# Transformer layers on one core: x and the first weights loaded in order of use, key products ahead of the compression, three gate tiles inside the last merge

## The chip, the cores and the metric

The kernel runs on one core of a Trainium2 chip. The metric is device time in microseconds (us) of one execution, the median of several runs.

## The reference, cut to what matters

Two transformer blocks follow each other over one sequence of 512 tokens with 1024 features, all in float32.

```python
def first_block(x, ...):                       # D = 1024, S = 512
    h = rms_norm(x, attn_norm_w)
    x = x + token_mixer(h, ...)                # retention, short convolution, sparse attention
    h = rms_norm(x, ffn_norm_w)
    x = x + conv_glu_ffn(h, ...)
    return rms_norm(x, final_norm_w)

def nsa_attention(...):                        # the sparse attention of the token mixer
    kc = compress(kc_raw, cmp_pos[0], cmp_w1[0], cmp_w2[0])   # blocks of 32 keys -> one
    vc = compress(vc_raw, cmp_pos[1], cmp_w1[1], cmp_w2[1])
    # heads attend to kc/vc, to selected keys ks/vs, and to a window kw/vw

def second_block(x, ...):
    h = rms_norm_2(x, attn_norm)
    # y_dn: gated delta rule branch; y_swa: sliding window branch
    gates = sigmoid(gate_raw)                  # 2 x 1024 columns: 16 tiles of 128
    merged = gates[0] * (y_dn @ w_branch_dn) + gates[1] * (y_swa @ w_branch_swa)
    x = x + merged @ w_out
    return x + (silu(h2 @ w_gate) * (h2 @ w_up)) @ w_down
```

## The kernel before, in words

Activations are held feature-major: 128 features on the partitions, 512 tokens in a row, eight such tiles for 1024 features. Every product runs in float32r as three matmuls, on a high and a low part of each factor: `split` makes the high part on ScalarE (ACT, L269 or L272) and the low part on VectorE (DVE, L270 or L273). `weight` loads a weight tile over SyncE's (SP's) queue (L286) and splits it; the loaded tile `wf` has two buffers, its parts `wh` and `wl` have three. A `gemm` is eight weight tiles of 128 by 128, with three matmuls each (wh·xh, wh·xl, wl·xh): 24 matmuls of 512 columns on TensorE (PE). RMS norm is applied behind a product: R, a row broadcast of 1/rms, multiplies the results.

The program is written in order of computation, and a scheduler under the kernel orders every engine's instructions ahead of time; each engine then works through its own list in that order. Tiles come from pools with a fixed number of buffers: in PSUM two each of `g`, `s` and `t`, and one each of `o` and `o2`. A load through `load` is issued by GpSimd (POOL) and keeps its place behind the last matmul written before it.

`setup` loads the norm vectors `vecs` and half of x over ACT's queue, the other half of x over POOL's, and the first weight tile in two halves over SP's. It splits x by tile, with the norm's weight as scale, computes the sum of squares (ACT squares, DVE adds to `acc`, PE sums the columns with `ones`), and `finish_norm` makes R of it through the reciprocal square root on DVE (L341 to L350) and four PE transposes (L372). The first product `nsa_raw_keys` has four gemms (the raw keys and values to be compressed, `w_kcvc`); for each result, ACT and DVE copy four half tiles into K2 (L486, L487).

Then come `nsa_compress` (per side 16 additions on DVE at L458, twice 16 small matmuls into `o`, a gelu on ACT and DVE at L465 to L472 whose result `zz` feeds a last small product) and `nsa_keys` (four gemms `w_kswk`, then the token-major products for the values, `w_vs` and `w_vw`).

In the second block `gates2` computes the 16 gate tiles (gemm, times R, tanh) into units of memory: 8 and 9 ahead of the delta rule, 10 to 15 behind its scan, and two behind each pair of the eight sliding-window heads (0 to 7). `merge` then runs twice. Per tile it has a gemm of half depth (12 matmuls, 256 KB of weights), DVE multiplies it by the gate (L841) and POOL adds it to `merged` in the second merge (L842). `split_all` splits merged (L272, L273) for the product with `w_wo`.

Of the kernel before, what the change touches and what calls it, by code (L numbers as in the profile page):

```python
# [8 lines left out]
F32 = mybir.dt.float32  # L9
# [3 lines left out]
OP = mybir.AluOpType  # L13
# [12 lines left out]
PITCH = 8 * (16 * 128 + 16)  # L26

# [169 lines left out]
class Kern:  # L197
# [92 lines left out]

    def gemm(self, w, xh, xl, nk=KD, p=None):
# [117 lines left out]
    def setup(self):  # L409
        nc, A = self.nc, self.A  # L410
        self.vecs = self.cp.tile([128, V_N], F32, name="vecs")
        nc.scalar.dma_start(self.vecs, A["vecs"])
        x = self.units(KD)
        for k in range(KD):
            (nc.scalar if k % 2 else nc.gpsimd).dma_start(x(k), A["xT"][:, k, :])
        first = self.weight(A["w_kcvc"][0], 2)
# [4 lines left out]
        for k in range(KD):  # L421
            self.split(xh(k), xl(k), x(k), self.vec(NORM1 + k))
        self.xh, self.xl = xh, xl
        self.consts = {}
        self.load_consts(0)
        self.load_consts(1)
        self.rows = self.cp.tile([128, R_N - R_DNO], F32, name="rows")
        self.load(self.rows, A["rows"][:, R_DNO:R_N].to_broadcast([128, R_N - R_DNO]))
# [46 lines left out]
    def nsa_raw_keys(self):  # L475
        nc, A = self.nc, self.A
        self.K2, self.cw = [], []
        for which in range(2):
            K = self.unit(shape=(128, 4, 512))
            for pair in range(2):  # L480
                p = self.gemm(A["w_kcvc"][which * 2 + pair], self.xh, self.xl, KD, self.pss() if which else None)
                t = self.scaled(p)
                for s in range(2):
                    rows = slice(64 * s, 64 * s + 64)
                    g = 2 * pair + s
                    nc.scalar.activation(K[0:64, g, :], t[rows, :], AF.Copy)  # L486
                    nc.vector.tensor_copy(K[64:128, g, 0:511], t[rows, 1:512])  # L487
# [35 lines left out]
    def nsa_keys(self):  # L523
# [913 lines left out]
```

## Time and profile before

| what | value |
|---|---|
| median of 3 runs | 2039.32 us (2038.29 to 2039.98) |
| the profiled execution | 2040.16 us |
| its span | 2038.4 us |
| PE busy | 2009.6 us |
| DVE busy | 1206.2 us |
| ACT busy | 837.6 us |
| POOL busy | 227.6 us |

The span runs from the first to the last recorded instruction of the profiled execution; 1.8 us of its time lie around it. PE is busy for nearly all of it, so the rows to look at are those in front of which PE stood still, and those of the engine that it waited for. In a timeline a row holds: start (us), length (us), engine, line, operation, what is written from what, shape, count, and in brackets the idle time before it and what ended that.

### The profile page before, as it was taken

What the parts mean: (1) busy time and instruction counts of PE and PEld (TensorE: products, weight loads), DVE (VectorE), ACT (ScalarE), POOL (GpSimd) and SP (SyncE); (2) the same over time, 40 slices, a digit from 0 to 9 for tenths busy, and PEclk for the clock granted to TensorE, in tenths of its full rate; (3) what the DMA queues carried; (4) which work ended last, traced back from release to release, by engine and by line L of the source; (5) the groups of instructions that cost most, each with busy time, mean ns of one, the idle gap of its engine ahead of it and who ended that gap; (6) DMA issues with size and microseconds to landing.
All of it is one profiled execution on the core that took longest, in us unless ns stands there. A gap on an engine that the chain in (4) does not pass through costs nothing.

```text
span 2038.4 us, 26002 instructions
## 1 busy us (share of the span) xinstructions
PE 2009.6 (99%) x9800; PEld 1669.1 (82%) x9800; DVE 1206.2 (59%) x2250; ACT 837.6 (41%) x1514; POOL 227.6 (11%) x336
## 2 busy tenths in 40 slices
PE   7999999999999999999999999999999999999999
PEld 6888888888888888888888888879878878888887
DVE  7477887854525645467767544784576764444322
ACT  4466776742122323334444332643544332232211
POOL 3000000000201111111111100011000211111100
PEclk9999999999999999999999999999999999999999
DMA  6122111122242232443333343321221353323442
GB/s 236 54 73 62 43 43 62 53 82 95 93 119 77 74 102 83 123 156 95 93 104 94 116 137 110 104 81 48 83 64 42 102 176 94 103 93 96 127 124 78
DMA packets 61837, 193.33 MB, mean 95 GB/s; under 512 B 10909, under 2 KB 13221, under 8 KB 61200
## 3 DMA queue, kind: packets, MB, share of 16 engines
q1 hardware_dynamic: 54336, 166.32, 26.5%
q0 software_dynamic: 6656, 24.17, 3.7%
q8 instruction: 77, 1.26, 0.2%
q10 hardware_dynamic: 720, 1.19, 0.2%
q14 instruction: 48, 0.39, 0.1%
HBM read 182.07 MB, written 9.58 MB: 94 GB/s over the span
## 4 chain that ended last, share of the span: by engine, by line
PE 89%; DVE 5%; ACT 3%; DMA 2%; issue 1%; ACTq 0%; POOL 0%; SPq 0%; DVEq 0%
PE g L263 73%; PE o L263 5%; PE s L263 5%; PE t L263 2%; PE t L676 2%; DVE wl L270 1%; ACT wh L269 1%; DMA u<-in_xT 1%; DVE st L573 0%; DVE sm L635 0%; DVE u L273 0%; DVE w L440 0%; ACT PT L665 0%; PE t L1334 0%; PE t L728 0%
## 5 line engine op out<-in xcount | busy, mean ns | idle before, releaser
L263 PE MATMUL g<-u,wh 128*128 128x512 f32 x4464 | 1402.2, 392 | 11.9 <-ACT u L272 10.1
L263 PEld LDWEIGHTS g<-u,wh 128*128 128x128 f32 x4464 | 834.6, 188 | 181.2 <-ACT u L272 11.2
L263 PE MATMUL g<-u,wl 128*128 128x512 f32 x2232 | 874.5, 392 | 0.2 <-DVE wl L270 0.2
L269 ACT ACTIVATE wh<-wf 128x1024 fp32r<-128x1024 f32 (+3 forms) x325 | 331.7, 1021 | 812.9 <-PE g L263 572.5
L270 DVE TENSOR_TENSOR wl<-wf,wh 128x1024 fp32r<-128x1024 f32 (+3 forms) x325 | 403.3, 1241 | 214.6 <-ACT wh L269 211.2
L263 PEld LDWEIGHTS g<-u,wl 128*128 128x128 f32 x2232 | 420.0, 188 | 84.5 <-DVE wl L270 1.2
L405 DVE TENSOR_TENSOR w<-g,R 128x512 f32<-128x512 f32 x104 | 71.5, 688 | 113.3 <-PE g L263 113.2
L440 DVE SCALAR_TENSOR_TENSOR w<-w,vecs 128x510 f32<-128x510 f32 (+1 forms) x140 | 104.6, 747 | 3.2 <-ACT w L438 0.8
L263 PE MATMUL o<-u 128*128 128x256 f32 (+1 forms) x418 | 78.0, 288 | 2.3 <-issue 1.4
L263 PE MATMUL g<-wh,u 128*128 128x512 f32 (+3 forms) x320 | 79.9, 330 | 0.0
L263 PE MATMUL s<-u,st 128*128 128x256 f32 (+2 forms) x288 | 73.3, 342 | 0.3 <-DVE mn L635 0.2
L263 PEld LDWEIGHTS o<-u 128*128 128x128 f32 x418 | 61.1, 189 | 12.8 <-ACT u L269 4.5
L269 ACT ACTIVATE u<-t 128x512 fp32r<-128x512 f32 (+1 forms) x112 | 56.1, 531 | 23.0 <-PE t L676 10.4
L1367 POOL TENSOR_TENSOR w<-w,R 128x512 f32<-128x512 f32 x22 | 39.0, 1773 | 198.5 <-ACT w L1366 198.5
L272 ACT ACTIVATE u<-w 128x512 fp32r<-128x512 f32 x44 | 27.4, 624 | 77.9 <-POOL w L889 77.9
L273 DVE SCALAR_TENSOR_TENSOR u<-w,u 128x512 fp32r<-128x512 f32 x44 | 30.4, 690 | 47.7 <-ACT u L272 47.7
L263 PEld LDWEIGHTS g<-wh,u 128*128 128x128 f32 x320 | 54.8, 189 | 4.2 <-DVE w L745 0.3
L263 PEld LDWEIGHTS s<-u,st 128*128 128x128 f32 x288 | 46.7, 189 | 10.4 <-issue 3.9
L263 PE MATMUL g<-wl,u 128*128 128x512 f32 (+3 forms) x160 | 52.6, 329 | 0.0
L438 ACT ACTIVATE w<-w,vecs 128x512 f32<-128x512 f32 x64 | 46.2, 722 | 13.8 <-DVE w L405 13.3
L889 POOL TENSOR_TENSOR w<-w 128x512 f32<-128x512 f32 x22 | 28.3, 1288 | 208.7 <-DVE w L440 208.7
L861 DVE TENSOR_TENSOR st<-st,g 128x512 f32<-128x512 f32 x24 | 16.5, 688 | 44.1 <-PE g L263 44.1
(388 smaller groups left out, 2036.8 us busy)
## 6 DMA issues: line engine op xcount, KB each, us to landing
wf<-in_w_fu SPq DMA_DIRECT2D x44, 512.0 KB, 3.5
wf<-in_x_gu SPq DMA_DIRECT2D x44, 512.0 KB, 3.6
wf<-in_w_sc SPq DMA_DIRECT2D x24, 512.0 KB, 3.5
wf<-in_w_mg SPq DMA_DIRECT2D x24, 512.0 KB, 3.5
wf<-in_w_fd SPq DMA_DIRECT2D x16, 512.0 KB, 3.7
wf<-in_x_gt SPq DMA_DIRECT2D x16, 512.0 KB, 3.5
wf<-in_x_dn SPq DMA_DIRECT2D x16, 512.0 KB, 3.7
x<-st POOLq DMA_DIRECT2D x24, 256.0 KB, 2.4
```

What stands on the lines that cost most here:

```text
L263: self.last = self.nc.tensor.matmul(out, l, r, start=start, stop=stop)
L269: nc.scalar.activation(hi, src, AF.Copy)
L270: nc.vector.tensor_sub(lo, src, hi.bitcast(F32))
L272: nc.scalar.activation(hi, src, AF.Copy, scale=scale)
L273: return nc.vector.scalar_tensor_tensor(lo, src, scale, hi.bitcast(F32), op0=OP.mult, op1=OP.subtract)
L405: self.nc.vector.tensor_mul(t, p, self.R)
L438: nc.scalar.activation(dst, src, AF.Copy, scale=self.vec(w + (nt - 1) * stride + j))
L440: nc.vector.scalar_tensor_tensor(dst[:, i:], src[:, :T - i], self.vec(w + (nt - 1 - i) * stride + j), dst[:, i:], op0=OP.mult, op1=OP.add)
L676: nc.tensor.transpose(pt[:, c:c + 128], parts[v][:, k * 128:(k + 1) * 128], self.ident)
L861: nc.vector.tensor_add(r, r, p)
L889: nc.gpsimd.tensor_mul(a, a, v)
L1367: nc.gpsimd.tensor_mul(t, t, self.R)
```

## The change

`setup`: only the eight columns of the first norm's weights (`n1`) are loaded over ACT's queue. x goes over SP's queue together with the first weight tile, in order of use: first half of the weight, x tiles 0 to 2, second half, x tiles 3 to 7. The splits are written in the same order. `vecs`, the constants and `rows` are loaded over POOL's queue behind a small copy that waits for the low part of x tile 4.

`block1`: `nsa_keys` (its four gemms) stands ahead of `nsa_compress`; the token-major products are now `nsa_values`, behind it. The second copy into K2 moves from DVE to ACT.

`block2`: after the scan only gates 10 to 12 are computed; the window heads take 13 to 15 and 0 to 4; gates 5, 6 and 7 are computed inside the second merge. In that merge the last three additions go to DVE in place of POOL.

```diff
+    def weight_x(self, ap, load, split):
...
+        halves = slice(0, 512), slice(512, 1024)
+        for c, ks in zip(halves, ((0, 1, 2), (3, 4, 5, 6, 7))):
+            self.nc.sync.dma_start(wf[:, c], ap[:, c])
+            load(ks)
+        for c, ks in zip(halves, ((0, 1, 2), (3, 4, 5, 6, 7))):
+            self.split(wh[:, c], wl[:, c], wf[:, c])
+            for k in ks:
+                split(k)
+        return wh, wl
...
     def setup(self):
-        nc.scalar.dma_start(self.vecs, A["vecs"])
+        nc.scalar.dma_start(n1, A["vecs"][:, NORM1:NORM1 + KD])
         x = self.units(KD)
-        for k in range(KD):
-            (nc.scalar if k % 2 else nc.gpsimd).dma_start(x(k), A["xT"][:, k, :])
-        first = self.weight(A["w_kcvc"][0], 2)
+        xd = lambda ks: [nc.sync.dma_start(x(k), A["xT"][:, k, :]) for k in ks]
...
-        for k in range(KD):
-            self.split(xh(k), xl(k), x(k), self.vec(NORM1 + k))
+        first = self.weight_x(A["w_kcvc"][0], xd, lambda k: self.split(xh(k), xl(k), x(k), n1[:, k:k + 1]))
...
+        self.last = nc.gpsimd.tensor_copy(self.vecs[:, 0:1], xl(4)[:, 0:1].bitcast(F32))
+        self.load(self.vecs, A["vecs"], self.last)
...
     def nsa_raw_keys(self):
-                    nc.vector.tensor_copy(K[64:128, g, 0:511], t[rows, 1:512])
+                    nc.scalar.activation(K[64:128, g, 0:511], t[rows, 1:512], AF.Copy)
...
     def merge(self, gates, out_w, yh, yl, merged, first, nk=KD):
-                nc.gpsimd.tensor_add(merged(n), merged(n), th)
+                add = nc.vector if nk < KD and n >= LATE else nc.gpsimd
+                add.tensor_add(merged(n), merged(n), th)
...
     def block1(self):
         self.nsa_raw_keys()
+        self.nsa_keys()
         self.nsa_compress()
-        self.nsa_keys()
+        self.nsa_values()
...
     def gates2(self, g, ns):
-            if n % 8 == 0:
-                self.gu = self.units(8)
+            if n in (0, 8):
+                self.gu = self.units(8 if n else LATE)
...
     def block2(self, x2, acc, acc2):
-        self.gates2(gates, range(10, 16))
+        self.gates2(gates, range(10, 13))
...
-            self.gates2(gates, range(2 * j, 2 * j + 2))
+            self.gates2(gates, ((13, 14), (15, 0), (1, 2), (3, 4))[j])
...
-        self.merge(lambda n: gates[n], A["x_bd"], yh, yl, merged, False, 4)
+        self.merge(lambda n: gates[n] if n < LATE else self.gate(A["x_gt"][n]), A["x_bd"], yh, yl, merged, False, 4)
```

LATE is 5. Three places show what moves. The first is SP's list at the start of the program (wf is the loaded weight tile, u a tile of x). Before:

```order
L286 DMA wf<-in_w_kcvc 128x512 x2
L286 DMA wf<-in_w_kcvc 128x1024 x3
L286 DMA wf<-in_w_kswk 128x1024 x4
L286 DMA wf<-in_w_vs 128x1024 x2
L286 DMA wf<-in_w_vw 128x912 x2
```

And now:

```order
L300 DMA wf<-in_w_kcvc 128x512
L431 DMA u<-in_xT 128x512 x3
L300 DMA wf<-in_w_kcvc 128x512
L431 DMA u<-in_xT 128x512 x5
L287 DMA wf<-in_w_kcvc 128x1024 x3
```

All eight tiles of x have moved into this queue, ahead of the second weight tile.

The second is PE's list at the first half of the compression (`o<-u` are its first 16 matmuls of one half, `o<-zz,st` its last product; `g<-u,wh` belongs to a gemm of the key products, `g<-wh,u` to the token-major product `w_vs`). Before:

```order
L263 MATMUL g<-u,wh 128x512
L263 MATMUL o<-u 128x128 x16
L263 MATMUL g<-u,wh 128x512
L263 MATMUL g<-u,wl 128x512
L263 MATMUL o<-u 128x128 x16
L263 MATMUL g<-u,wh 128x512 x2
...
L263 MATMUL o<-zz,st 128x128 x2
```

And now:

```order
L264 MATMUL o<-u 128x128 x16
L264 MATMUL g<-wh,u 128x256
L264 MATMUL g<-wl,u 128x256
L264 MATMUL g<-wh,u 128x256 x2
L264 MATMUL o<-u 128x128 x16
L264 MATMUL g<-wl,u 128x256
L264 MATMUL g<-wh,u 128x256 x2
L264 MATMUL g<-wl,u 128x256
L264 MATMUL o<-zz,st 128x128
```

It stood in the second key gemm; it now stands at the start of `w_vs`, with all four key gemms ahead of it.

The third is DVE's list at the end of the second merge (`wl` is a weight split, `u<-u,s`, `w<-w,s` the product with the gate, `w<-g,R` the new gate's scaling, `u<-u,w` the addition, `u<-u` the low part of merged, `st` belongs to the product behind it). Before:

```order
L270 TENSOR_TENSOR wl<-wf,wh 128x1024
L841 SCALAR_TENSOR_TENSOR u<-u,s 128x512
L273 SCALAR_TENSOR_TENSOR u<-u 128x512
L270 TENSOR_TENSOR wl<-wf,wh 128x1024
L273 SCALAR_TENSOR_TENSOR u<-u 128x512
L1401 SCALAR_TENSOR_TENSOR st<-st,vecs,R_10286 128x512
```

And now:

```order
L422 TENSOR_TENSOR w<-g,R 128x512
L271 TENSOR_TENSOR wl<-wf,wh 128x1024
L862 SCALAR_TENSOR_TENSOR w<-w,s 128x512
L274 SCALAR_TENSOR_TENSOR u<-u 128x512
L864 TENSOR_TENSOR u<-u,w 128x512
L271 TENSOR_TENSOR wl<-wf,wh 128x1024
L274 SCALAR_TENSOR_TENSOR u<-u 128x512
```

The addition has joined DVE's list between the last product with the gate and the last low part.

## Rows read from the trace of the kernel before

**Rows 1.** The page's first part: busy time, share of the span, instructions.

```profile
PE 2009.6 (99%) x9800; PEld 1669.1 (82%) x9800; DVE 1206.2 (59%) x2250; ACT 837.6 (41%) x1514; POOL 227.6 (11%) x336
```

**Rows 2.** Who PE waited for, whole span: total us, times, longest us.

```profile
PE g L263 <- ACT u L272: 10.1, 3, 8.3
...
PE o L263 <- DVE PT L1338: 0.7, 1, 0.7
...
PE o L263 <- ACT PT L1340: 0.4, 1, 0.4
```

**Rows 3.** Timeline of the start, all engines (the columns are explained above).

```profile
5.57 0.63 ACT L269 ACTIVATE wh<-wf 128x512 fp32r<-128x512 f32 x1 [0.40 <-DMA wf<-in_w_kcvc]
...
15.36 0.72 ACT L272 ACTIVATE u<-u,vecs 128x512 fp32r<-128x512 f32 x1 [1.63 <-DMA u<-in_xT]
...
16.11 0.75 DVE L273 SCALAR_TENSOR_TENSOR u<-u,vecs 128x512 fp32r<-128x512 f32 x1 [1.56 <-ACT u L272]
...
24.22 1.48 DVE L385 TENSOR_TENSOR acc<-acc,sm 128x512 f32<-128x512 f32 x2
...
25.76 1.05 PE L263 MATMUL o<-ones,acc 128*128 128x1 f32 x8 [0.77 <-DVE acc L385]
...
29.04 0.16 DVE L350 SCALAR_TENSOR_TENSOR rsr<-rsa,rsy 128x4 f32<-128x4 f32 x1
...
31.99 0.61 PE L263 MATMUL s<-u,wh 128*128 128x512 f32 x2
...
35.39 0.61 PE L263 MATMUL s<-u,wh 128*128 128x512 f32 x2
```

**Rows 4.** Two stretches of the start; the last two columns are DMA share and GB/s.

```profile
2.30:5.30 3.00, 0.00 (x0) 0.00 (x0) 0.34 (x3) 1.91 (x2) 2.96 (x7) 1.00 0.98 325
...
9.00:13.50 4.50, 4.50 (x14) 3.05 (x14) 3.11 (x6) 3.07 (x5) 0.00 (x0) 1.00 1.03 393
```

**Rows 5.** Tile wf, first 45 us: ns min/median/max, first and last start.

```profile
L269 ACT ACTIVATE wh<-wf x8: 629/1050/1069, 4.5 to 36.8; 128x1024 fp32r<-128x1024 f32 x6, 128x512 fp32r<-128x512 f32 x2
L270 DVE TENSOR_TENSOR wl<-wf,wh x8: 692/1218/1226, 5.2 to 39.0; 128x1024 fp32r<-128x1024 f32 x6, 128x512 fp32r<-128x512 f32 x2
L286 SPq DMA_DIRECT2D wf<-in_w_kcvc x5: 327/387/424, 0.8 to 18.3; - x5
```

**Rows 6.** DMA issues: count, KB each, median us from issue to landing.

```profile
wf<-in_x_bs SPq DMA_DIRECT2D x8, 256.0 KB, 2.6
```

**Rows 7.** Timeline of the compression, all engines.

```profile
44.70 4.02 PE L263 MATMUL o<-u 128*128 128x128 f32 x32 [1.44 <-issue]
...
62.33 3.84 PE L263 MATMUL o<-u 128*128 128x128 f32 x32 [0.43 <-ACT w L465]
...
64.27 0.23 DVE L472 TENSOR_SCALAR zz<-w 128x128 f32<-128x128 f32 x1
...
67.46 0.73 PE L263 MATMUL g<-u,wh 128*128 128x512 f32 x2 [0.49 <-DVE w L535]
```

**Rows 8.** Timeline of the copies into K2, ACT.

```profile
32.24 2.56 ACT L486 ACTIVATE u<-w 64x512 f32<-64x512 f32 x4
```

**Rows 9.** A stretch inside `w_vs` and `w_vw`: us, PE busy (count), PEld busy.

```profile
85.00:104.00 19.00, 19.00 (x144) 19.00 (x143) 5.63 (x9) 6.97 (x13) 0.00 (x0) 1.00 0.18 56
```

**Rows 10.** Timeline of the second merge's end, all engines.

```profile
1628.35 0.67 DVE L841 SCALAR_TENSOR_TENSOR u<-u,s 128x512 f32<-128x512 f32 x1
...
1629.12 1.65 POOL L842 TENSOR_TENSOR u<-u 128x512 f32<-128x512 f32 x1 [1.22 <-DVE u L841]
...
1631.48 0.50 PE L263 MATMUL g<-u,wh 128*128 128x512 f32 x1 [1.06 <-ACT u L272]
...
1632.51 0.50 PE L263 MATMUL g<-u,wh 128*128 128x512 f32 x1 [0.53 <-DVE u L273]
```

**Rows 11.** Two stretches behind it; the third column from the end is the granted clock.

```profile
1632.50:1636.30 3.80, 3.79 (x10) 2.98 (x11) 3.33 (x5) 2.30 (x3) 1.08 (x2) 0.60 0.72 251
1636.30:1640.30 4.00, 4.00 (x18) 3.27 (x17) 0.43 (x1) 0.11 (x1) 0.00 (x0) 0.95 0.70 208
```

More of the change, by code (lines that the diff above doesn't have):

```diff
@@ L26 @@
 PITCH = 8 * (16 * 128 + 16)
+LATE = 5
 NORM1, NORM_F1, NORM_FIN, NORM2, NORM_F2 = 0, 8, 16, 24, 32
@@ L289, in weight @@
         return wh, wl
+    def weight_x(self, ap, load, split):
+        ap = ap.rearrange("p k c -> p (k c)")
+        wf = self.wp.tile([128, 1024], F32, name="wf", bufs=2)
+        wh = self.wp.tile([128, 1024], F32R, name="wh", bufs=3)
+        wl = self.wp.tile([128, 1024], F32R, name="wl", bufs=3)
+        halves = slice(0, 512), slice(512, 1024)
[7 more added lines that the diff above has]
+        return wh, wl
     def gemm(self, w, xh, xl, nk=KD, p=None):
@@ L410, in setup @@
         nc, A = self.nc, self.A
-        self.vecs = self.cp.tile([128, V_N], F32, name="vecs")
-        nc.scalar.dma_start(self.vecs, A["vecs"])
+        n1 = self.cp.tile([128, KD], F32, name="n1")
+        nc.scalar.dma_start(n1, A["vecs"][:, NORM1:NORM1 + KD])
         x = self.units(KD)
-        for k in range(KD):
-            (nc.scalar if k % 2 else nc.gpsimd).dma_start(x(k), A["xT"][:, k, :])
-        first = self.weight(A["w_kcvc"][0], 2)
+        xd = lambda ks: [nc.sync.dma_start(x(k), A["xT"][:, k, :]) for k in ks]
         self.ones = self.cp.tile([128, 1], F32, name="ones")
@@ L420, in setup @@
         acc = self.accum()
-        for k in range(KD):
-            self.split(xh(k), xl(k), x(k), self.vec(NORM1 + k))
+        self.vecs = self.cp.tile([128, V_N], F32, name="vecs")
+        self.rows = self.cp.tile([128, R_N - R_DNO], F32, name="rows")
+        first = self.weight_x(A["w_kcvc"][0], xd, lambda k: self.split(xh(k), xl(k), x(k), n1[:, k:k + 1]))
         self.xh, self.xl = xh, xl
         self.consts = {}
[L425 to L428, printed above, removed]
+        self.last = nc.gpsimd.tensor_copy(self.vecs[:, 0:1], xl(4)[:, 0:1].bitcast(F32))
+        self.load(self.vecs, A["vecs"], self.last)
+        for c in range(2):
+            self.load_consts(c)
+        self.load(self.rows, A["rows"][:, R_DNO:R_N].to_broadcast([128, R_N - R_DNO]), self.last)
         self.ident = self.const("ident")
@@ L521, in nsa_compress, with nsa_values, ev, ev_s @@
         self.pbuf, self.pn = ((b[1], b[2]), (b[0], b[3])), 0
+    def nsa_values(self):
+        nc, A = self.nc, self.A
+        xh, xl = self.xh, self.xl
+        self.V = [self.unit(F32R, (128, 4, 4, 128)) for _ in range(2)]
+        self.gates = self.cp.tile([128, 4, 48], F32, name="gates")
+        def ev(br, t, p):
+            src = p[:, :256].rearrange("p (g d) -> p g d", g=4)
+            hi, lo = self.V[br][:, t, :, 0:64], self.V[br][:, t, :, 64:128]
+            r = self.r[:, t:t + 1]
+            nc.scalar.activation(hi, src, AF.Copy, scale=r)
+            nc.vector.scalar_tensor_tensor(lo, src, r, hi.bitcast(F32), op0=OP.mult, op1=OP.subtract)
+        def ev_s(t, p):
+            ev(0, t, p)
+        def ev_w(t, p):
+            ev(1, t, p)
+            nc.scalar.activation(self.gates[:, t, :], p[:, 256:304], AF.Tanh, scale=self.rh[:, t:t + 1])
+        self.gemm_nat(A["w_vs"], 256, xh, xl, ev_s)
+        self.gemm_nat(A["w_vw"], 304, xh, xl, ev_w)
+        nc.vector.tensor_scalar(self.gates, self.gates, 0.5, 0.5, op0=OP.mult, op1=OP.add)
+        self.y = self.units(8)
     def nsa_keys(self):
@@ L541, in nsa_keys @@
                     nc.vector.tensor_sub(KL[rows, s, :], t[rows, :], KH[rows, s, :].bitcast(F32))
-        self.V = [self.unit(F32R, (128, 4, 4, 128)) for _ in range(2)]
-        self.gates = self.cp.tile([128, 4, 48], F32, name="gates")
-        def ev(br, t, p):
-            src = p[:, :256].rearrange("p (g d) -> p g d", g=4)
-            hi, lo = self.V[br][:, t, :, 0:64], self.V[br][:, t, :, 64:128]
-            r = self.r[:, t:t + 1]
-            nc.scalar.activation(hi, src, AF.Copy, scale=r)
-            nc.vector.scalar_tensor_tensor(lo, src, r, hi.bitcast(F32), op0=OP.mult, op1=OP.subtract)
-        def ev_s(t, p):
-            ev(0, t, p)
-        def ev_w(t, p):
-            ev(1, t, p)
-            nc.scalar.activation(self.gates[:, t, :], p[:, 256:304], AF.Tanh, scale=self.rh[:, t:t + 1])
-        self.gemm_nat(A["w_vs"], 256, xh, xl, ev_s)
-        self.gemm_nat(A["w_vw"], 304, xh, xl, ev_w)
-        nc.vector.tensor_scalar(self.gates, self.gates, 0.5, 0.5, op0=OP.mult, op1=OP.add)
-        self.y = self.units(8)
     def nsa_query(self, j):
```

## The prediction

> **What bounds the kernel now.** I read the busy times first: PE is busy 2009.6 of 2038.4 us [rows 1]. The change takes no matmul out and adds none, so all it can win is time in which PE stands still or runs at the lower clock. The list of PE's waits comes next: the one large entry is 10.1 us for the first high parts of x, 8.3 of it in front of the first matmul [rows 2]. Then I read the timeline at the three places that the change touches: the start, where PE waits for x, for weight splits and for the column sum [rows 3]; the compression, with five waits of which the first is 1.44 and the last 0.49 us, 3.14 in all [rows 7]; and the end of the second merge, with waits of 1.06 and 0.53 us [rows 10], behind which the mean granted clock is 0.60, that is mostly the lower of its two levels, 1.2 in place of 2.4 GHz [rows 11]. The rate of everything else follows from two rows five k-steps apart: 3.40 us, so 0.68 us for three matmuls of 512 columns, 0.227 each [rows 3].
>
> **The start.** Before, eight x tiles, the weights and the constants are in flight together; DMA moved 325 to 393 GB/s [rows 4], and the last x tile's high part begins at 15.36 us [rows 3]. Now the x tiles go over SP's queue between the weight halves, and the constants wait for x tile 4. SP needs some 0.39 us for an issue [rows 5], and a 256 KB load lands 2.6 us behind its issue [rows 6]. At 325 to 393 GB/s the next ones land 0.67 to 0.81 us apart; I take 0.7. From the first issue at 0.8 us: weight half 3.4, x0 4.1, x1 4.8, and the tenth load, x7, at 9.7 us.
> ACT splits the half weight (0.63, rows 5), squares x0 (the list puts that ahead of the high part; same size, so again about 0.63), then makes the high parts at 0.72 [rows 3]. x0's is done at 5.4 us and PE begins there in place of 8.3 [rows 2].
> From there DVE sets the pace, not the loads: eight low parts at 0.75 [rows 3] and one weight half at 0.69 [rows 5] make 6.7 us, so x7's low part is done at 12.1 in place of 16.11 + 0.75 = 16.86. PE's lower clock in its first microseconds is hidden under that. Two additions to `acc` (1.48, rows 3) and the second weight's low part (1.22, rows 5) follow: PE has that at 14.8 us.
> Then the column sum. DVE still has five additions (3.7), one weight split (1.2) and four small operations (0.6) ahead of it: 20.3 us. PE reaches it after 20 more matmuls, 4.5 us, at 19.3, and waits 1.0. Before, the column sum began at 25.76 [rows 3], but with eight matmuls more behind it (1.8 us). So the gain here is 25.76 - 20.3 - 1.8 = 3.7 us.
> One step gives some of it back. DVE's list now has a weight split (fifth weight tile) between the mean and the reciprocal root, and its high part needs the buffer that the second gemm frees at about 21.8. That is 1.05 + 1.22 behind it, 24.1, and then the rest of a chain that took from 26.81 to 29.20 before [rows 3], some 2.1 us: 26.2. PE comes to the transposes at about 25.2 and waits 1.0. Behind it ACT waits with the next splits, and nobody waits for those. The start is thus worth 2.7 us. Its ends: 4.7 with neither wait, 1.0 if `rows` (issued last on POOL, and ACT's `al` waits for it ahead of three squares) comes 1.7 us late for the squares. I take 2.7, since it goes by rows.
>
> **The compression.** The four key gemms now stand ahead of it. The copies into K2, 16 on ACT at 0.64 [rows 8], make 10.2 us, with 16 copies of the keys as many again and eight splits at 1.05: 29 us of work in about 33 us of gemms, so ACT keeps up, without much room. The loads of the compression's weights land under the gemms. Of the five waits (3.14 us) all go. In their place the small product of the gelu waits: from the end of the 16 matmuls to `zz` it was 61.90 to 64.50, 2.6 us [rows 7]. PE's list has between them four or so matmuls of `w_vs`, the other half's product and then 11 to 12 more, at 19.0/144 = 0.13 us each [rows 9], 2.1 to 2.2 us. Twice 0.45 us is left: 0.9. The gain is 2.2 us; its ends are 3.1 (no new wait) and 0.5 (ACT late by a copy or two at each handing over).
>
> **The window heads and the scan.** Three gate gemms of 16.3 us move away from behind the scan. PE stood nowhere there, and the bias table has five gemms (27 us) to land. In the heads, gates 13 to 15 have their memory already, so their matmuls can stand between the first heads, where PE waited 0.67 and 0.41 us for the transposed weights [rows 2]. I take 0.8 us for it, with ends of +1.1 and, since every row of these 70 us is ordered anew and DVE is near its limit there, -1.5.
>
> **The second merge.** Before, DVE multiplies tile 7 at 1628.35, POOL adds until 1630.77, ACT and DVE split, and PE's next product stands still for 1.06 + 0.53 us [rows 10]. Behind that the clock is at half: 3.8 us at 0.60 and 4.0 at 0.95 [rows 11], so 1.5 + 0.2 = 1.7 us lost. Now three gate gemms of 5.45 us each stand in the merge, under which DVE catches up. Behind the last one comes, on DVE: product 0.67, low part 0.68, addition 0.74; on ACT the high part 0.63, done 2.8 us behind PE's last merge matmul with the handings over. The last low part is done at about 4.3 (a weight split is ahead of it). PE needs them at 7 x 0.68 = 4.8 us of the next gemm. So both waits go and the clock should stay: 3.3 us. If a wait of half a us is left the clock may still fall; then 1.1. What is added, three scalings and three tanh, is hidden by the half-depth gemm of 2.7 us behind each gate.
>
> **The sum.** 2.7 + 2.2 + 0.8 + 3.3 = 9.0 us. The profiled execution took 2040.16, so 2031.2 by it; it lies 0.84 above the median, so the median goes from 2039.3 to 2030.3.
>
> **Rivals.** A measurement of this kernel tells about 0.2% from no change, 4.1 us: the border is at 2035.2.
> (a) The start gives nearly nothing: PE's early work is now in pieces with waits of 0.5 to 1.0 us in front of the second gemm, the column sum and the transposes, and the clock falls as behind the merge, twice 1.7 us. Against it: after a single wait of 1.44 us [rows 7] no row shows a slower matmul; for it: 1.06 and 0.53 close together did it [rows 10, 11]. The start is then -0.7 and the sum 5.6: 2033.7. The Trainium skill ("TensorE: Matmul & The Clock Gate", "What's actually happening") says that the throttled clock is the default and that activity releases it, which is this rival's mechanism; the trace agrees with its direction at rows 11.
> (b) Within 0.2%: SP's queue alone does not carry what three queues carried. At half of 393 GB/s the ten loads, 2.6 MB, need 13.3 us; with the 1.9 that a load of 0.7 us takes beside its transfer [rows 6] and the first issue at 0.8, x7 lands at 16.0, about where it did, and the start is worth nothing; with one fall of the clock kept elsewhere (1.7) the rest makes 4.6 - the heads' 0.8, 3.8: 2035.5. Against it: 393 GB/s with loads of 256 to 512 KB [rows 4]. The Trainium skill ("DMA: Bandwidth & Descriptors", "Measured (HBM→SBUF, 128 partitions, SWDGE, issued from GpSimd)") asks for at least 1 MiB a load to reach three quarters of the peak, and speaks for this rival; rows 4 show more than it grants loads of this size, though not on one queue.
> (c) Slower: loads of one queue follow each other singly. Ten at 2.6 us [rows 6] put x7 at 26.8 and its split 11.4 us later than before; with the 6.3 of the other parts that is +5.1: 2044.4. It decides from 2.1 us a load on (1.46 a load is even at the start). Against it: the two weight halves went out over SP's queue at 0.8 and 1.2 us; one behind the other, the second would have landed at 0.8 + 2 x 2.6 = 6.0 at the earliest, and ACT began to split it at 5.57 [rows 3].
> (d) The change does what it says in the merge but DVE, now with the additions, is late for the weights there. Per late tile it has 1.22 + 0.69 + 0.69 + 0.67 + 0.68 + 0.74 = 4.7 us of work in 5.45 + 2.7 of PE's: it has room, so I give it no chance of its own.
>
> **How the numbers follow.** Forecast 0.64 (2026 to 2032.5), (a) 0.20, (b) 0.12, (c) 0.04. Low end: the parts at their best, 4.7 + 3.1 + 1.1 + 3.4 = 12.3, so 2027.0, and 0.5 for the 1.8 us around the span. High end: the start and the heads at their worst, 1.0 - 1.5, with the other two as forecast, 5.5, make 5.0, so 2034.3, and 1.2 more if ACT is late in the compression as well: 2035.5. That takes in (a) and leaves out half of (b), and (c). Faster by over 0.2%: 0.64 + 0.20 = 0.84; same 0.12; slower 0.04.
>
> **What would show it.** Right: first matmul near 5.4 us, x7's low part near 12, the column sum near 20, with a wait of about 1 there and at the transposes; one uninterrupted row of gemms to about 55 us; no wait over 0.3 us and a clock of 1.00 behind the second merge. Wrong: x tiles landing more than 1 us apart; a clock below 1.00 before 30 us; ACT's copies ending behind the key gemms; new waits for DVE among the window heads.

## The result and the profile after

The changed kernel takes 2028.34 us (median of 4 runs, 2027.90 to 2028.79) against 2038.99 us of the kernel before on the same chip: a ratio of 0.9947, 95% interval 0.9930 to 0.9965, 10.65 us less. The forecast was 2030.3 us. The two profiled spans lie further apart, 2038.4 and 2026.6 us, 11.8 us. The page of the changed kernel begins so; the busy times answer to [rows 1]:

```profile
span 2026.6 us, 26014 instructions
...
PE 2005.6 (99%) x9800; PEld 1668.6 (82%) x9800; DVE 1197.7 (59%) x2245; ACT 843.6 (42%) x1522; POOL 220.5 (11%) x331
```

Where the 11.8 us come from is read from operations on DVE that both programs have: the copy that makes R, the last operation on `gates` in the first block (all of the compression, the keys and the values lies between the two), the mean of the heads' sums, the last head's last product, and the second addition behind the merge. Between them, in us; in the column after, the three gate gemms that moved (72 matmuls, 16.36 us) are added back to the third stretch and taken off the fifth:

| stretch | before | after | gain | forecast |
|---|---|---|---|---|
| start, to R | 30.35 | 26.85 | 3.50 | 2.7 |
| R to `gates` (compression) | 75.98 | 74.40 | 1.6 | 2.2 |
| `gates` to the heads' sums | 1397.29 | 1397.18 | 0.1 | 0 |
| the eight heads | 69.85 | 67.58 | 2.3 | 0.8 |
| heads to behind the merge | 66.90 | 62.81 | 4.1 | 3.3 |
| rest | 398.03 | 397.78 | 0.2 | 0 |

Over the runs below, a stretch that an edit doesn't touch comes out within 0.3 us of these (the rest once 0.5 us shorter), with two exceptions: R lies between 26.45 and 27.56 us in the kernels that share the new start, and the third stretch varies by up to 0.8 us, and by more in two runs, where it is told.

The list of PE's waits in the changed kernel (engine, line, for what: total, times, longest) answers to [rows 2]. In front of the first matmul 6.2 us are left of 8.3, and the waits for `PT` in the heads are gone; new is 1.6 us for `w` in the compression.

```profile
PE g L264 <- ACT u L273: 6.2, 1, 6.2
PE o L264 <- ACT w L482: 1.6, 1, 1.6
...
PE g L264 <- DVE wl L271: 0.6, 1, 0.6
```

PE's timeline of the start (columns as ahead of the prediction), against [rows 3]: two short waits are left, and none at the column sum (20.49) and the transposes (26.18).

```profile
6.17 1.58 PE L264 MATMUL g<-u,wh 128*128 128x512 f32 x2 [6.17 <-ACT u L273]
...
14.25 0.73 PE L264 MATMUL g<-u,wh 128*128 128x512 f32 x2 [0.37 <-ACT wh L270]
...
15.58 0.50 PE L264 MATMUL g<-u,wl 128*128 128x512 f32 x1 [0.60 <-DVE wl L271]
...
20.49 1.05 PE L264 MATMUL o<-ones,acc 128*128 128x1 f32 x8
...
26.18 0.62 PE L389 MATMUL o<-c,rsr 128*128 128x128 f32 x4
```

In the compression, against [rows 7], all five old waits are gone, and the one new wait stands between the two halves of the first product:

```profile
61.07 3.84 PE L264 MATMUL o<-u 128*128 128x128 f32 x32 [1.64 <-ACT w L482]
```

Behind the second merge PE has no wait of 0.1 us or more. The window (PE, PEld, DVE, ACT and POOL busy, granted clock, DMA share, GB/s) shows the clock at 1.00, where [rows 11] had 0.60:

```profile
1624.00:1630.00 6.00, 6.00 (x29) 4.95 (x28) 3.57 (x6) 2.76 (x5) 1.28 (x3) 1.00 0.55 176
```

### The profile page after: what moved, and what is told of

Read it like the earlier page. It is cut to its first block, busy times and chain, and to the rows that moved or that the text cites. A ratio compares the mean times of both kernels' runs of the same rounds, so it can differ in the third digit from the quotient of the medians.

```text
span 2026.6 us, 26014 instructions
## 1 busy us (share of the span) xinstructions
PE 2005.6 (99%) x9800; PEld 1668.6 (82%) x9800; DVE 1197.7 (59%) x2245; ACT 843.6 (42%) x1522; POOL 220.5 (11%) x331
## 3 DMA queue, kind: packets, MB, share of 16 engines
q8 instruction: 77, 1.26, 0.3%
## 4 chain that ended last, share of the span: by engine, by line
PE 92%; DVE 4%; ACT 2%; DMA 1%; issue 1%; ACTq 0%; SPq 0%; DVEq 0%
PE g L264 75%; PE s L264 6%; PE o L264 5%; PE t L264 2%; PE t L697 2%; DVE wl L271 1%; ACT wh L270 1%; DVE st L594 0%; DVE sm L656 0%; DVE w L457 0%; DMA u<-in_xT 0%; PE t L1357 0%; ACT PT L686 0%; PE t L749 0%; PE t L1186 0%
## 5 line engine op out<-in xcount | busy, mean ns | idle before, releaser
L422 DVE TENSOR_TENSOR w<-g,R 128x512 f32<-128x512 f32 x107 | 73.5, 688 | 117.1 <-PE g L264 116.9
L862 DVE SCALAR_TENSOR_TENSOR w<-w,g 128x512 f32<-128x512 f32 x17 | 11.7, 688 | 53.4 <-PE g L264 50.0
```

The lines of the kernel that those rows point to most:

```text
L422: self.nc.vector.tensor_mul(t, p, self.R)
L862: self.order.append(nc.vector.scalar_tensor_tensor(th, th, 1.0, p, op0=OP.add, op1=OP.mult))
```

## The experiments

Each run is the changed kernel with one edit. The times are medians of 5 to 8 runs; the kernel before took 2038.5 to 2038.9 us beside them, and 2038.99 us beside the changed kernel. So a difference of half a us in the last column says nothing by itself.

| run | edit | us | against 2028.34 |
|---|---|---|---|
| r1_start_old | start as before | 2030.69 | +2.4 |
| r2_keys_old | compression ahead of the keys, as before | 2032.88 | +4.5 |
| r3_adds_pool | all additions of the merge on POOL | 2028.12 | -0.2 |
| r4_gates_old | no gates in the merge | 2032.48 | +4.1 |
| r5_k2_dve | second K2 copy on DVE | 2032.32 | +4.0 |
| r6_heads_order | the eight gates of the heads in another order | 2031.14 | +2.8 |
| r7_o2 | second half of the product in its own bank | 2026.82 | -1.5 |
| r8_warm | eight idle matmuls ahead of the first | 2032.32 | +4.0 |
| r9_unit | gate 0 early instead of gate 12 | 2028.63 | +0.3 |
| r10_x_queues | x over ACT's and POOL's queues | 2029.49 | +1.2 |
| r11_consts_early | constants not held back | 2030.00 | +1.7 |
| r12_o2_square | r7_o2, x0's square held back | 2027.08 | -1.3 |

### Are the four parts independent? The start and the compression undone

```diff
-        xd = lambda ks: [nc.sync.dma_start(x(k), A["xT"][:, k, :]) for k in ks]
+        for k in range(KD):
+            (nc.scalar if k % 2 else nc.gpsimd).dma_start(x(k), A["xT"][:, k, :])
+        first = self.weight(A["w_kcvc"][0], 2)
...
```

> The changed kernel with the start of the kernel before: all loads in flight together, constants not held back, x0's square behind the high parts. Theory (the gain is the sum of four parts that don't touch each other: start 3.3, compression 1.9, window heads 2.3, second merge 4.0 us, as the two traces lie apart at the same matmul): the changed kernel's 2028.3 + 3.3 = 2031.6 us, the first matmul back at 8.3 us, and the compression, the heads and the merge as far apart as in the changed kernel. Rival (the parts share a slack: with the keys ahead of the compression there are 33 us of gemms in which the vector and scalar engines catch up, so a late start is partly absorbed, or the compression's wait of 1.64 us changes with it): 2029 to 2030.5, or above 2032.5.

```diff
-        self.nsa_keys()
         self.nsa_compress()
+        self.nsa_keys()
...
-                    nc.scalar.activation(K[64:128, g, 0:511], t[rows, 1:512], AF.Copy)
+                    nc.vector.tensor_copy(K[64:128, g, 0:511], t[rows, 1:512])
```

> The changed kernel with the compression again ahead of the key gemms, and the second copy into K2 again on the vector engine. Theory of four separate parts: 2028.3 + 1.9 = 2030.2 us, the waits of the compression back (3.1 us in five pieces), the wait of 1.64 us for the copy of the product o gone. Rival (the new start gave the compression its weights and tables earlier, or later since the constants are held back, so the old order would not show the old waits): under 2029.5 or over 2031.5.

Neither came out as the theory of separate parts has it. The two traces and those of the kernels before and after make a square; in it stands when the operation on `gates` begins:

| | compression first | keys first |
|---|---|---|
| start of before | 106.33 | 103.56 |
| new start | 105.25 | 101.24 |

The new start alone is worth 1.1 us, the new order alone 2.8, both together 5.1. (The second K2 copy goes with the order: on DVE with the compression first, on ACT with the keys first.) The reason is a different one on each side. With the compression first, its first product waits for a chain on DVE from R over the K2 copies to the first additions. That chain takes 14.35 us in both kernels (26.93 to 41.28; before, 30.35 to 44.70); in r2_keys_old DVE ends the last copy at 40.8 us and begins the first addition there, while the weights that this product needs have landed by 36.6. But the new start brings PE there 5.0 us earlier (38.24 in place of 43.26) and R only 3.4. So PE waits 3.04 us in place of 1.44, and the clock falls behind it: the same 32 matmuls take 5.46 us in place of 4.02 [rows 7]. PE's row and two windows of r2_keys_old:

```profile
41.28 5.46 PE L264 MATMUL o<-u 128*128 128x128 f32 x32 [3.04 <-issue]
```

```profile
41.20:44.00 2.80, 2.72 (x17) 2.75 (x18) 2.80 (x13) 0.00 (x0) 0.12 (x1) 0.69 0.96 382
44.00:47.00 3.00, 3.00 (x19) 2.78 (x18) 0.72 (x4) 0.22 (x1) 0.00 (x0) 0.72 0.02 7
```

With the keys first, R is 3.6 us later in r1_start_old than in the changed kernel, but the stretch behind it is 1.26 us shorter, since the wait of 1.64 us is 0.54 there. The order of ACT's list differs: one of the two weight splits of the values stands behind the four key copies in place of ahead of them. ACT in r1_start_old (57.36 is ahead of the copies, 62.39 behind them), and then in the changed kernel, where both are ahead:

```profile
57.36 1.06 ACT L270 ACTIVATE wh<-wf 128x1024 fp32r<-128x1024 f32 x1
59.78 0.63 ACT L581 ACTIVATE u<-w 64x512 fp32r<-64x512 f32 x1 [1.35 <-DVE w L577]
...
62.39 0.96 ACT L270 ACTIVATE wh<-wf 128x912 fp32r<-128x912 f32 x1
63.26 0.26 ACT L482 ACTIVATE w<-o 128x128 f32<-128x128 f32 x1
```

```profile
55.33 1.91 ACT L270 ACTIVATE wh<-wf 128x1024 fp32r<-128x1024 f32 x2
58.28 0.63 ACT L581 ACTIVATE u<-w 64x512 fp32r<-64x512 f32 x1 [1.04 <-DVE w L577]
...
60.76 0.25 ACT L482 ACTIVATE w<-o 128x128 f32<-128x128 f32 x1
```

The heads and the merge are the same in both runs as in the changed kernel (67.5 to 67.8 and 62.9 us), so these two parts are independent of the others.

### What makes the new wait in the compression

```diff
-                    nc.scalar.activation(K[64:128, g, 0:511], t[rows, 1:512], AF.Copy)
+                    nc.vector.tensor_copy(K[64:128, g, 0:511], t[rows, 1:512])
```

> The changed kernel, its keys ahead of the compression, but the second copy into K2 back on the vector engine (it takes 1.07 us there, 0.63 on ACT; eight of them). It tells whether ACT's amount of work makes the wait of 1.64 us in the compression (ACT has 8 x 0.63 = 5.0 us less to do, the vector engine 8.5 us more). Theory (ACT is late since it does the 32 copies): the wait falls under 0.6 us, 2027.0 to 2027.8 us. Rival (ACT isn't full there, it waits 1.0 to 2.0 us for the vector engine's scaling of each key tile, so the vector engine's list is what is late): the wait stays or grows, new waits of PE for weight splits, 2028.5 to 2031 us.

```diff
         for hh in range(2):
-            p = self.ps("o", 1)
+            p = self.ps("o2" if hh else "o", 1)
```

> The changed kernel with the second half of each compression product in an accumulator of its own (bank o2 in place of o), so that PE needn't wait until ACT has copied the first half out. Theory (the wait of 1.64 us is for that copy and nothing else stands behind it): the wait goes, 1.2 to 1.6 us less, 2026.7 to 2027.1 us. Rival (the wait moves: ACT and the vector engine reach the gelu of the second half as late as before, and PE waits for it or for the splits of the values' weights): 2028.0 to 2028.6 us, with a new wait of 1 us or more between 61 and 70 us.

ACT's amount of work is not it. With 5 us less of it, the wait grows to 3.50 us, since DVE then brings the scaled key tile later and ACT stands 4.08 us for it. And again the clock falls behind the wait: 0.50, then 0.88. PE, ACT and two windows of r5_k2_dve:

```profile
62.81 5.20 PE L264 MATMUL o<-u 128*128 128x128 f32 x32 [3.50 <-ACT w L482]
```

```profile
54.47 0.63 ACT L581 ACTIVATE u<-w 64x512 fp32r<-64x512 f32 x1 [4.08 <-DVE w L577]
```

```profile
62.80:65.00 2.20, 2.19 (x10) 2.19 (x11) 1.32 (x5) 0.31 (x1) 0.00 (x0) 0.50 0.32 116
65.00:68.00 3.00, 3.00 (x26) 3.00 (x26) 0.00 (x0) 0.00 (x0) 0.00 (x0) 0.88 0.00 0
```

What PE waits for is the bank. The first half of the product ends in `o` at 59.4 us, and the second half needs the same bank, which ACT empties only behind the four copies of the last key tile. With a bank of its own for the second half the wait is gone, and two of 0.39 and 0.35 us for the gelu take its place; R to `gates` is 72.57 in place of 74.40 us. PE in r7_o2:

```profile
62.54 0.46 PE L264 MATMUL o<-zz,st 128*128 128x128 f32 x2 [0.39 <-ACT w L482]
...
72.45 0.41 PE L264 MATMUL o<-st,zz 128*128 128x64 f32 x2 [0.35 <-DVE zz L489]
```

At 2026.82 us (ratio 0.9943, 0.9931 to 0.9955) this is, with r12_o2_square, which has the same edit, the fastest kernel of the study. Its five runs, 2025.87 to 2026.99, all lie below the lowest of the changed kernel's, 2027.90. But the kernel before was 0.5 us faster beside it too, so about 1 us of the 1.5 is left, and the intervals of the two ratios overlap; that the stretch is 1.83 us shorter is read from the traces.

### The merge: gates inside it, or additions on DVE

```diff
-                add = nc.vector if nk < KD and n >= LATE else nc.gpsimd
-                add.tensor_add(merged(n), merged(n), th)
+                nc.gpsimd.tensor_add(merged(n), merged(n), th)
```

> The changed kernel with all eight additions of the second merge on POOL; the three gates stay inside it. Theory (the gate gemms in the merge give the vector engine its time; the additions' engine matters little): no wait over 0.3 us behind the merge, granted clock 1.00 there, 2028.3 to 2028.8 us. Rival (the last addition's engine decides: 1.65 us on POOL against 0.69 on the vector engine, and a split that runs beside POOL's addition takes 1.78 in place of 0.68): a wait of about 1 us for the last halves of the merged tiles, the clock falls behind it, 2029.5 to 2031.5 us.

```diff
-        self.gates2(gates, range(10, 13))
+        self.gates2(gates, range(10, 16))
...
-            self.gates2(gates, ((13, 14), (15, 0), (1, 2), (3, 4))[j])
+            self.gates2(gates, range(2 * j, 2 * j + 2))
...
```

> The changed kernel with the gates where they were (six ahead of the heads, two behind each pair of heads, none inside the merge) and the additions of tiles 5 to 7 still on the vector engine. The heads' 2.3 us go back in any case, so 2030.6 us at least. Theory (the gates inside the merge do it): the waits at the end of the merge stay, 0.8 to 1.6 us, and the clock falls behind them: 2031.5 to 2034.6 us. Rival (the additions alone do it, since a split beside POOL's addition takes 1.78 in place of 0.68 us and the last addition 1.65 in place of 0.69): waits under 0.3 us, clock 1.00 behind the merge, 2030.4 to 2031.0 us.

With the gates in the merge, the additions' engine is worth nothing: 62.81 us in both. POOL's last addition takes 1.66 us, and a split beside it 2.31 in place of 1.22, but DVE has that time. DVE and POOL of r3_adds_pool:

```profile
1618.79 0.69 DVE L862 SCALAR_TENSOR_TENSOR w<-w,s 128x512 f32<-128x512 f32 x1 [0.65 <-PE s L264]
...
1620.00 2.31 DVE L271 TENSOR_TENSOR wl<-wf,wh 128x1024 fp32r<-128x1024 f32 x1
```

```profile
1619.57 1.66 POOL L863 TENSOR_TENSOR u<-u,w 128x512 f32<-128x512 f32 x1 [5.94 <-DVE w L862]
```

Without the gates the additions alone take the merge from 66.90 to 64.24 us: one wait of 1.00 is left of 1.06 + 0.53 [rows 10], and the clock stays at 1.00. So both sides were partly right. DVE is the limit there: from 1613.1 to 1628.0 us it has no idle time of 0.1 us, and the splits beside POOL's additions take 1.78 us each in place of 0.68. PE, DVE, POOL and a window of r4_gates_old:

```profile
1628.04 0.50 PE L264 MATMUL g<-u,wh 128*128 128x512 f32 x1 [1.00 <-DVE u L274]
```

```profile
1616.12 1.78 DVE L274 SCALAR_TENSOR_TENSOR u<-u 128x512 fp32r<-128x512 f32 x1
...
1627.30 0.68 DVE L274 SCALAR_TENSOR_TENSOR u<-u 128x512 fp32r<-128x512 f32 x1
```

```profile
1615.52 1.83 POOL L864 TENSOR_TENSOR u<-u 128x512 f32<-128x512 f32 x1 [1.23 <-DVE u L862]
```

```profile
1628.10:1632.00 3.90, 3.90 (x17) 3.24 (x18) 2.98 (x4) 2.20 (x3) 1.08 (x2) 1.00 0.62 210
```

(The profiled execution of this run also lost 1.4 us between `gates` and the heads' sums, which the edit doesn't touch; it has a wait of 1.11 us at 1364 us there.) The Trainium skill ("GPSIMD Engine Reference", "1. Specifications") says that POOL shares its interface to SBUF with DVE and contends with DVE instructions that have two operands in SBUF; the splits are of that kind, and 2.31 against 1.22 us agrees. The slow split of 1.78 us ends 0.55 us behind the end of POOL's addition, and that of 2.31 us 1.08 us behind it: nearly their undisturbed lengths, 0.68 and 1.22. The extra time is about the rest of POOL's addition.

### The heads: which gates stand among them

```diff
-            self.gates2(gates, ((13, 14), (15, 0), (1, 2), (3, 4))[j])
+            self.gates2(gates, ((0, 1), (2, 3), (4, 13), (14, 15))[j])
```

> The changed kernel with the same eight gates among the heads in another order: 0 to 3 behind the first two pairs of heads, 4 and 13 behind the third, 14 and 15 behind the fourth; 5 to 7 stay in the merge. The order of matmuls among the heads is then that of the kernel before. Theory (gates 13 to 15 have their memory early, so their matmuls can stand among the first heads, and that is worth the 2.3 us): 2028.3 + 2.3 = 2030.6 us, the waits of 0.67 and 0.41 us behind the first head back, the merge as in the changed kernel. Rival (fewer gates' values held or the shorter row of six gemms ahead of the heads does it, or the start of the heads falls better to the bias table's load): 2028.0 to 2028.8 us.

```diff
...
-                self.gu = self.units(8 if n else LATE)
-            g[n] = self.gu(n % 8)
+                gu = self.units(8 if n else LATE)
+                self.gu = (self.gu[0], gu) if n == 0 else (gu, None)
+            g[n] = self.gu[n < 8](n % 8)
...
-        self.gates2(gates, range(10, 13))
+        self.gates2(gates, (10, 11, 0))
...
-            self.gates2(gates, ((13, 14), (15, 0), (1, 2), (3, 4))[j])
+            self.gates2(gates, ((1, 2), (3, 12), (13, 14), (15, 4))[j])
```

> The changed kernel with gates 10, 11 and 0 ahead of the heads and, behind the pairs of heads, (1, 2), (3, 12), (13, 14), (15, 4). Results of four gates share one unit of memory, 12 to 15 one and 0 to 3 one. Theory (what counts is that the first gates behind a head write into a unit which an earlier gate has opened: their scaling can then stand ahead of the first head's last operations on the vector engine, and both accumulators g come free): gates 1 and 2 find the unit that gate 0 opened, the time is the changed kernel's, 2028.0 to 2028.8 us, and PE shows no wait behind the first head. Rival (it is gates 13 to 15 and their place in the list that count): the 2.3 us go back as in the run with gates 0 and 1 first, 2030.3 to 2031.2 us, with waits of 0.66 and 0.40 us.

In r6_heads_order the heads take 69.83 us, as before the change (69.85), and both waits are back. In r9_unit they take 67.57, as in the changed kernel. So neither the number of gates among the heads nor the gates 13 to 15 as such count, but whether the first gate of the heads writes into a unit of memory that another gate has opened. DVE shows what that changes: in r6_heads_order the first two scalings (L422) stand behind the last product of the first head (L1372), in the changed kernel ahead of it, the first by 12 us. Until they are done both banks `g` are full and no third gate can fill PE's gaps. PE and DVE of r6_heads_order, then DVE of the changed kernel:

```profile
1497.38 1.10 PE L264 MATMUL o<-u,PT 128*128 128x64 f32 x8 [0.66 <-DVE PT L1361]
...
1499.70 0.88 PE L264 MATMUL o<-u,PT 128*128 128x64 f32 x6 [0.40 <-ACT PT L1363]
```

```profile
1498.52 0.42 DVE L1372 TENSOR_TENSOR u<-o,swd 128x256 f32<-128x256 f32 x1 [0.35 <-PE o L264]
...
1499.45 0.68 DVE L422 TENSOR_TENSOR u<-g,R 128x512 f32<-128x512 f32 x1
1500.18 0.68 DVE L422 TENSOR_TENSOR u<-g,R 128x512 f32<-128x512 f32 x1
```

```profile
1486.67 0.68 DVE L422 TENSOR_TENSOR u<-g,R 128x512 f32<-128x512 f32 x1
...
1493.86 0.68 DVE L422 TENSOR_TENSOR u<-g,R 128x512 f32<-128x512 f32 x1
...
1498.75 0.42 DVE L1372 TENSOR_TENSOR u<-o,swd 128x256 f32<-128x256 f32 x1
```

Why a first write into a new unit comes so late was not tried: the memory may still have been in use, or the scheduler alone may have put it there.

### The start: what of it is the queue, the held constants, the clock, the square

```diff
-        xd = lambda ks: [nc.sync.dma_start(x(k), A["xT"][:, k, :]) for k in ks]
+        xd = lambda ks: [(nc.scalar if k % 2 else nc.gpsimd).dma_start(x(k), A["xT"][:, k, :]) for k in ks]
```

> The changed kernel with the x tiles on ACT's and POOL's queues in turn, as before the change, the weight halves alone on SP's, the constants still held back. It tells whether one queue's order of use is what makes the start. Theory (the vector engine's low parts set the pace from the first matmul to 13 us, so how x gets there matters little as long as nothing else is in flight): first matmul within 0.4 us of 6.2, column sum within 0.4 us of 20.5, 2027.9 to 2028.8 us. Rival (three queues issue at once, so all eight tiles share the bandwidth with the first weight half and x0 lands late): first matmul 1 us later or more, 2029 to 2030 us.

```diff
-        self.last = nc.gpsimd.tensor_copy(self.vecs[:, 0:1], xl(4)[:, 0:1].bitcast(F32))
-        self.load(self.vecs, A["vecs"], self.last)
+        self.load(self.vecs, A["vecs"])
...
```

> The changed kernel with the vectors, both sets of constants and the rows loaded at once over POOL's queue instead of behind x tile 4's low part (0.6 MB in flight beside x). Theory (holding them back is a part of the start's gain, since 0.6 MB at 380 GB/s are 1.6 us of transfer ahead of or among x): x tiles land up to 1.6 us later, first matmul 6.5 to 7.5 us, the column sum up to 1 us later, 2028.5 to 2029.8 us. Rival (the vector engine's pace covers it, and the waits of 0.44 us for the rows and 0.7 us for the vectors go instead): 2027.8 to 2028.5 us.

Three queues at once are the worse way: the first high part of x waits 2.14 us for its tile, the first matmul comes at 8.22 us as before the change, and R at 29.07 in place of 26.85. (The stretch of the compression wins 1.8 of these 2.2 us back, with a wait of 0.41 in place of 1.64; the median is 1.2 us up.) Constants in flight leave the first matmul where it was, but DVE waits 1.22 and 1.45 us for the high parts of the next tiles, and R comes at 28.93. In both, DVE's last addition to `acc` ends late by itself (24.2 and 22.5 us against 20.4), so the loads explain the delay without PE's rate, which rose later here too (at 13.1 and 16.0 us, see the last section). Each half of the new order of loads is thus worth some 2 of the 3.5 us at R, and they overlap. PE of r10_x_queues, DVE of r11_consts_early:

```profile
8.22 1.58 PE L264 MATMUL g<-u,wh 128*128 128x512 f32 x2 [8.22 <-ACT u L273]
...
24.26 1.05 PE L264 MATMUL o<-ones,acc 128*128 128x1 f32 x8 [0.83 <-DVE acc L402]
```

```profile
8.09 0.75 DVE L274 SCALAR_TENSOR_TENSOR u<-u,n 128x512 fp32r<-128x512 f32 x1 [1.22 <-ACT u L273]
10.29 0.75 DVE L274 SCALAR_TENSOR_TENSOR u<-u,n 128x512 fp32r<-128x512 f32 x1 [1.45 <-ACT u L273]
```

```diff
+        wm = self.tmp(tag="PT")
+        nc.vector.memset(wm, 1.0)
+        pw = self.pst()
+        for i in range(8):
+            nc.tensor.matmul(pw, wm[:, 0:128].bitcast(F32R), wm.bitcast(F32R), start=True, stop=True)
```

> The changed kernel with eight matmuls of 512 columns added whose result nobody uses, on a tile of ones, before x has landed, so that PE's granted clock is up when the first real matmul begins (in the changed kernel it is at its lower level until 9.9 us). Theory (from 6.2 to 15 us the vector engine's low parts set the pace, so PE's lower clock there costs nothing): 2028.1 to 2028.6 us, PE's waits for low parts longer, the end of the second weight's low part unmoved at 15.5 us. Rival (the clock costs: 3.7 us at half speed are up to 1.9 us): 2026.5 to 2027.5 us, the column sum unmoved but PE ahead of it. Other side: the added matmuls hold back the first real one, 2029 us or more.

This one didn't do what it was made for. PE works from 1.51 us on, but behind a stop of 0.82 us the first real matmuls run as slowly as without it (0.43 us apart up to 10.0 us, 0.23 from there, in both kernels). (The column of the granted clock reads 1.00 there in both; the lower level that the expectation names is read from these distances.) So it doesn't tell what that rate costs; R lies at 26.60, inside the spread of this start. Its median of 2032.32 is that of two groups (2029.0 to 2030.2 and 2034.5 to 2035.6 us, four runs each): the profiled one, of the upper group, has a wait of 1.58 us at 1389.6 us, far from the edit, and behind it the clock is at half for most of 12 us. PE and windows of r8_warm:

```profile
1.51 3.78 PE L439 MATMUL t<-PT 128*128 128x512 f32 x8 [1.51 <-DVE PT L436]
6.11 1.58 PE L264 MATMUL g<-u,wh 128*128 128x512 f32 x2 [0.82 <-ACT u L273]
```

```profile
1391.20:1395.00 3.80, 3.80 (x23) 3.62 (x24) 1.84 (x3) 1.06 (x1) 0.73 (x1) 0.70 0.47 158
1395.00:1399.00 4.00, 4.00 (x19) 3.81 (x19) 0.98 (x3) 0.60 (x1) 0.00 (x0) 0.50 0.45 131
```

```diff
-        for k in range(KD):
+        self.after(nc.scalar.activation(acc[0], x(0), AF.Square), self.low)
+        for k in range(1, KD):
             self.square_add(acc, k, x(k))
```

> The second half of the compression product in bank o2 (2026.8 us) and, beside it, x0's square held behind x tile 4's low part, so that x0's high part is the second thing ACT does. Theory (the vector engine's chain from x0's low part to the column sum is what the start waits for, and the square of 0.6 us stands in front of it): first matmul 5.5 us, column sum 0.3 to 0.6 us earlier, 2026.2 to 2026.6 us. Rival (the square only moves: the additions to the sum start later, the column sum stays where it is and with it all that follows): 2026.7 to 2027.0 us. Other side: the scheduling of the additions behind it changes for the worse, 2027.2 us or more.

The scheduler put the square of x1 into the place that x0's left, so ACT waited for x1 and made x0's high part at 6.56 in place of 5.42. The question of the square stays open. (`self.low` is the low part of x tile 4.) Nor does the run tell what the first matmul itself counts: it comes 1.25 us later than in r7_o2 (7.32 in place of 6.07) and R 0.89 us later (27.34), which is still inside the spread of this start, while the median is only 0.26 us higher, less than the 0.41 us by which the kernel before was slower beside it. ACT in r12_o2_square:

```profile
6.03 0.63 ACT L398 ACTIVATE sm<-u 128x512 f32<-128x512 f32 x1 [1.60 <-DMA u<-in_xT]
6.56 1.93 ACT L273 ACTIVATE u<-u,n 128x512 fp32r<-128x512 f32 x3
```

## Why the prediction was right, and which of its steps were not

**The sum.** 9.0 us were forecast and 10.65 measured, 11.8 by the spans. Sign and size hold. The order of the parts doesn't: the heads, last in the forecast, brought more than the compression. Three terms came out larger than forecast and one smaller; that the compression's shortfall of 0.6 us offsets a part of the others' surplus is luck. And the sum treated the parts as independent, and two of them aren't: the square above gives 1.1 + 2.8 for the start and the order of the compression one at a time and 5.1 for both. The terms could be added up only because each was costed in the finished change, the compression with its keys ahead.

**The start (2.7; 3.5 at R).** The ends of the chain were nearly right: the column sum was forecast at 20.3 us and begins at 20.49, the reciprocal root at 26.2 and ends at 26.1. In between two steps were off. The first matmul came at 6.17, not 5.4: the first weight half landed at 4.00 in place of 3.4, and ACT then waited 0.25 us for x0. x2 came 0.51 us late for ACT as well, and x7's low part was done at 13.0 in place of 12.1. And the two waits of 1 us, at the column sum and the transposes, didn't come. At the column sum PE itself was later, since the second weight's low part came at 15.5 in place of 14.8 and PE then had 20 matmuls to do. At the transposes PE was later too: six steps of three matmuls of the third gemm stand ahead of them, so it came there at 26.18 and not at 25.2. The giving back that was forecast there (a split between the mean and the root) did take place; it had nobody waiting. One reading was off without harm: of the 10.1 us that PE waited for high parts [rows 2], 1.06 belong to the merge's end [rows 10] and not to x.

**The compression (2.2; 1.6).** All five waits went, as forecast. What was to take their place did not: the gelu shows no wait of 0.2 us. Instead the lower end of the term came true in part, "ACT late by a copy or two": 1.64 us for the copy out of `o`. The step that failed is the one on ACT's room. It was reckoned from amounts of work (29 of 33 us), but ACT has idle time there, and the order of its list and one bank decide, as r5_k2_dve and r7_o2 show.

**The heads (0.8; 2.3, above the upper end of 1.1).** The mechanism was right: gates 13 to 15 have their memory already, and r6_heads_order and r9_unit show that it is the open unit that counts. The size was not. The term was bounded by the recorded waits, 0.67 + 0.41, but some 1.0 of the 2.3 us stands in no wait: the same 404 matmuls are recorded as 68.26 us busy in r6_heads_order and as 67.29 in the changed kernel, since in the older order they lie further apart. The Trainium skill ("Perfetto Trace Analysis", "Identifying the Most-Contended Engine") says that the busy share of matmuls is no good measure of how close a kernel is to its limit, because pipelined matmuls look smaller in the trace. This stretch agrees that it misleads, though here it is the larger busy time that hides a loss. The heads in r6_heads_order, then in the changed kernel (columns as above):

```profile
1482.70:1552.50 69.80, 68.26 (x404) 56.10 (x403) 53.84 (x130) 37.18 (x102) 2.40 (x8) 1.00 0.15 45
```

```profile
1482.07:1549.65 67.58, 67.29 (x404) 55.97 (x404) 53.48 (x130) 37.64 (x102) 2.39 (x8) 1.00 0.15 47
```

**The merge (3.3; 4.1).** Waits of 1.59 us and 1.7 us of clock were forecast, and both went. DVE's catching up under the gate gemms is what does it, as forecast (r3_adds_pool). The additions on DVE, which the forecast put on its side of the sum, would alone have brought 2.7 us (r4_gates_old; that it is by ending the slow splits beside POOL fits the rows there, but wasn't tried apart); on top of the gates they bring nothing. The remaining 0.8 us stand beside the two waits of before: from its matmul at 1629.32 to the one at 1633.08 us PE makes six steps in 3.76 us, which at 0.227 each would be 1.36. So 2.4 us are lost there, and 1.59 of them are recorded as waits. PE of the kernel before:

```profile
1629.32 0.86 PE L263 MATMUL g<-u,wh 128*128 128x512 f32 x2
...
1633.08 0.89 PE L263 MATMUL g<-u,wh 128*128 128x512 f32 x2
```

**The rivals.** (a) The clock doesn't fall at the start; the waits there are 0.37 and 0.60 us. (b) One queue carries x: DMA moves 379 GB/s from 6 to 10 us, above half of 393 by far, and three queues are slower (r10_x_queues). (c) falls with it. The window, with columns as above:

```profile
6.00:10.00 4.00, 3.83 (x8) 2.74 (x9) 3.41 (x5) 3.46 (x7) 0.00 (x0) 1.00 1.02 379
```

## What to carry to other kernels

A recorded wait is a lower bound of what an engine loses in a stretch with many small handings over; compare the time between two operations that both programs have, not the sum of the waits. Where a wait is for an accumulator, ask who empties it and what stands ahead of that on its engine's list: a second bank was worth more than 5 us less of work. Two edits on one chain are tried one at a time and together before their gains are added.

## What the runs showed of the hardware that was not expected

The clock fell to its lower level behind one wait of 3.04 us, one of 3.50, one of 1.58 (12 us behind one of 1.13), and, before the change, behind 1.06 and 0.53 close together; behind single waits of 1.64 us (changed kernel), 1.58 (r9_unit) and 1.00 (r4_gates_old) it stayed at 1.00. So among waits of about 1.6 us a wait's own length doesn't tell whether the clock will fall; the fall then cost 1.4 to 1.7 us in the compression and the merge and some 5 us in r8_warm. At the very start the matmuls of the changed kernel run at about half rate for 3.8 us behind the first one (0.43 us apart, then 0.23 from 10.0 us on) while the clock's column reads 1.00, so that column doesn't show this stretch. How long it lasts differs between runs with the same start: in r2_keys_old the rate rises at 11.7 us, in r9_unit at 12.7. In r12_o2_square, whose matmuls stand 0.43 us apart from 8.7 us on, it rises at 13.8. Whether this makes a part of the spread of R was not tried.
